# Both products of a feed-forward block by one level of Strassen's recursion, the down product as a phase of its own

## The chip, the core and the metric

The kernel runs on one core of one Trainium2 chip. The metric is the device time of one execution in microseconds: 1386.5, 1390.3 and 1393.4 us in three runs of the kernel before, a median of 1390.3. Engines are named as the profile names them: PE (TensorE matmul) with PEld (its weight loads), DVE (VectorE), ACT (ScalarE), POOL (GpSimd) and SP (SyncE), which here only issues DMAs.

## The reference

The reference is a transformer block on 1024 frames of width 1024 with 16 meta tokens ahead of them: a mixer (retention and attention heads with an output projection), then a gated feed-forward part with a short convolution, then a final norm. The change touches the end of the mixer's output projection, the feed-forward part and the final norm:

```python
def conv_ffn(h, w_up, conv_w, conv_b, w_down, valid):
    up = jnp.einsum('bld,df->blf', h, w_up)
    a, b = jnp.split(up, 2, axis=-1)
    a = a * valid.astype(a.dtype)[None, :, None]
    a_pad = jnp.pad(a, ((0, 0), (CONV_W - 1, 0), (0, 0)))
    acc = conv_b
    for j in range(CONV_W):
        acc = acc + a_pad[:, j:j + L] * conv_w[j]
    return jnp.einsum('blf,fd->bld', jax.nn.silu(acc) * b, w_down)
```

with `h = h + conv_ffn(rms_norm(h, ffn_norm_g), ...)` and `rms_norm(h, final_norm_g)` after it. Everything is float32.

## The kernel before

Activations lie transposed: the 1024 model features are 8 tiles (d or k, 0 to 7) of 128 partitions, the frames are columns. NQ is 1026 columns: the 1024 frames (NF) and the two tokens ahead of them that the convolution needs. The feed-forward width 2816 is 22 tiles (ft) of 128.

PE multiplies in the type fp32r, which keeps fewer digits than float32. So every operand is split into a high part (a cast, on ACT) and a low part (the difference, on DVE or POOL), and each product is three matmuls: high by high, high by low, low by high. Every matmul has its own weight load.

1. Rest of the output projection, in `rest_mm` (L1048): for each d in the order 6, 7, 0, ..., 5, matmuls of 342 columns, three to a row of NQ. Tiles 6 and 7 need all 8 k, the others the last two k, whose weights POOL splits on the way (`load_w`, L118). DVE adds the result to the residual H (`rest_h`, L1054); ACT and DVE make the two halves of H times the norm's weight, `hss` (L1055, L1058); squares are summed in `acc2` (L1063 to L1067).
2. Up product: `up_mm` (L1089) multiplies `hss`, not yet divided by its root mean square. `rstd` (L124 to L128) and a broadcast through DRAM give that factor, `rb2`, and DVE applies it when it reads the product out of PSUM (L1138 for a, L1150 for b). So PE can start the up product before the factor is known.
3. Per ft, `up` then does the convolution (L1141 on ACT, L1142 and L1143 on DVE), Silu (L1144), the gate (L1151) and the split of the result u (L1153, L1154), and loads and splits the down weights.
4. Down product: `down` (L1166 to L1168) multiplies the tile before, ft - 1, eight d by two halves of 512 columns, and DVE adds each result to H in SBUF (L1170). The last two tiles are left for the end, where the final norm works in column chunks of 512, 256 and 256.

The order inside a stage before step 2's loop is written out by hand (`manual_schedule`). From `up(0)` on the framework's scheduler sets the order of all engines. SP's order is the scheduler's throughout.

## Time and profile before

| | us |
|---|---|
| three runs | 1386.5, 1390.3, 1393.4 |
| profiled execution: span from first to last instruction | 1387.9 (the page gives no other time of it) |
| rest of the output projection, first matmul | 563.0 |
| feed-forward part, first matmul (L1089) | 612.1 |
| last down matmul (L1168) | 1368.9 |
| PE busy, DVE busy, ACT busy, POOL busy | 1339.2, 816.7, 464.6, 270.1 |

In the profile a matmul's duration overlaps that of its neighbours, so what a matmul costs in a dense stretch is read from start to start. A stretch of the span is read from a row of busy times: its length, then PE, PEld, DVE, ACT and POOL, the clock that PE was granted (1.00 is full), the busy share of the 16 DMA engines and GB/s. A wait is put down to the instruction that released it.

### The profile page before, as it was taken

What the parts mean: (1) busy time and instruction counts of PE and PEld (TensorE: products, weight loads), DVE (VectorE), ACT (ScalarE), POOL (GpSimd) and SP (SyncE); (2) the same over time, 40 slices, a digit from 0 to 9 for tenths busy, and PEclk for the clock granted to TensorE, in tenths of its full rate; (3) what the DMA queues carried; (4) which work ended last, traced back from release to release, by engine and by line L of the source; (5) the groups of instructions that cost most, each with busy time, mean ns of one, the idle gap of its engine ahead of it and who ended that gap; (6) DMA issues with size and microseconds to landing.
All of it is one profiled execution on the core that took longest, in us unless ns stands there. A gap on an engine that the chain in (4) does not pass through costs nothing.

```text
span 1387.9 us, 20331 instructions
## 1 busy us (share of the span) xinstructions
PE 1339.2 (96%) x8257; PEld 1225.0 (88%) x8257; DVE 816.7 (59%) x1400; ACT 464.6 (33%) x825; POOL 270.1 (19%) x177
## 2 busy tenths in 40 slices
...
GB/s 291 158 97 111 33 74 75 25 65 99 70 95 80 137 154 88 199 83 61 31 46 46 46 46 46 49 59 46 47 55 52 50 56 47 46 46 46 16 0 122
DMA packets 45237, 103.89 MB, mean 75 GB/s; under 512 B 7951, under 2 KB 18527, under 8 KB 45144
## 3 DMA queue, kind: packets, MB, share of 16 engines
...
## 4 chain that ended last, share of the span: by engine, by line
PE 82%; DVE 3%; issue 2%; ACT 2%; POOL 1%; DMA 0%; DVEq 0%; SPq 0%; POOLq 0%; ACTq 0%
PE psj L1089 18%; PE psv L1089 18%; PE psD L667 11%; PE psq L1167 6%; PE psq L1168 6%; PE psq L1166 6%; PE psO L825 4%; PE psD L895 4%; PE psS L788 3%; PE psS L731 2%; PE psj L1048 1%; PE psq L1048 1%; PE psj L185 1%; PE psj L184 1%; PE psj L183 1%
## 5 line engine op out<-in xcount | busy, mean ns | idle before, releaser
L1170 DVE TENSOR_TENSOR H<-H,psq 128x512 f32<-128x512 f32 (+1 forms) x344 | 229.3, 673 | 181.2 <-PE psq L1168 181.2
L1089 PE MATMUL psj<-hs,u_hi 128*128 128x342 f32 x1056 | 222.1, 322 | 2.0 <-ACT u_hi L117 2.0
L1089 PEld LDWEIGHTS psj<-hs,u_hi 128*128 128x128 f32 x1056 | 182.4, 190 | 15.9 <-ACT u_hi L117 2.4
L1089 PE MATMUL psv<-hs,u_hi 128*128 128x512 f32 x704 | 195.8, 398 | 0.0
L1089 PEld LDWEIGHTS psv<-hs,u_hi 128*128 128x128 f32 x704 | 134.1, 191 | 29.5
L1141 ACT ACTIVATE ca<-at,sm 128x1024 f32<-128x1024 f32 x22 | 25.4, 1154 | 369.8 <-DVE at L1138 369.8
L118 POOL TENSOR_TENSOR d_lo<-d_raw,d_hi 128x1024 fp32r<-128x1024 f32 x22 | 52.9, 2404 | 493.0 <-ACT d_hi L117 493.0
L1166 PE MATMUL psq<-u,d_hi 128*128 128x512 f32 (+1 forms) x368 | 141.0, 385 | 2.0 <-ACT u L1153 1.6
L1167 PE MATMUL psq<-u,d_hi 128*128 128x512 f32 (+1 forms) x368 | 141.1, 383 | 0.3 <-DVE u L1154 0.3
L1168 PE MATMUL psq<-u,d_lo 128*128 128x512 f32 (+1 forms) x368 | 141.1, 383 | 0.0
L667 PE MATMUL psD<-xl,f_hi 128*128 128x256 f32 (+2 forms) x448 | 129.7, 290 | 0.0
L667 PE MATMUL psD<-xh,f_hi 128*128 128x256 f32 (+2 forms) x448 | 128.8, 287 | 0.4 <-DVE fq L673 0.4
L667 PE MATMUL psD<-xh,f_lo 128*128 128x256 f32 (+2 forms) x448 | 128.5, 287 | 0.0
L118 POOL TENSOR_TENSOR u_lo<-u_raw,u_hi 128x1024 fp32r<-128x1024 f32 x44 | 107.2, 2437 | 76.0 <-ACT u_hi L117 68.4
L1089 PE MATMUL psv<-hs,u_lo 128*128 128x512 f32 x352 | 114.6, 395 | 0.0
L1089 PE MATMUL psj<-hs,u_lo 128*128 128x342 f32 x528 | 112.3, 320 | 1.0 <-POOL u_lo L118 1.0
L1150 DVE TENSOR_TENSOR bt<-psv,rb 128x512 f32<-128x512 f32 x44 | 28.4, 686 | 115.4 <-PE psv L1089 115.4
L1089 PEld LDWEIGHTS psj<-hs,u_lo 128*128 128x128 f32 x528 | 89.8, 189 | 5.1 <-POOL u_lo L118 1.3
L798 ACT ACTIVATE pf<-psS 128x272 f32<-128x272 f32 (+4 forms) x112 | 49.7, 451 | 116.4 <-PE psS L788 70.6
L667 PEld LDWEIGHTS psD<-xh,f_hi 128*128 128x128 f32 x448 | 85.3, 190 | 0.9 <-DVE fq L673 0.6
L667 PEld LDWEIGHTS psD<-xl,f_hi 128*128 128x128 f32 x448 | 85.0, 190 | 0.4
L667 PEld LDWEIGHTS psD<-xh,f_lo 128*128 128x128 f32 x448 | 85.0, 190 | 0.1
...
## 6 DMA issues: line engine op xcount, KB each, us to landing
...
```

The lines of the kernel that those rows point to most:

```text
L118: eng_lo.tensor_tensor(lo, src, f(hi), op=ALU.subtract)
L667: pe.matmul(ps[:, :n], lhsT=w_, rhs=X(e, k, t0 + a, n), start=(k == 0 and i == 0), stop=(k == KT - 1 and i == 2))
L788: pe.matmul(ps[:r, off:off + n], lhsT=k_[s][:, t0:t0 + r], rhs=q_[s][:, q0:q0 + n], start=(e == 0), stop=(e == 1 and not diag))
L798: act.activation(pf[:r, a:b], ps[:r, a:b], AF.Exp)
L825: pe.matmul(po[:, q0 - qs:qn], lhsT=v_, rhs=P2[:r, P_, off:off + n], start=(i == 0 and e == 0), stop=(fin and e == 2))
L895: pe.matmul(ps[:, :n], lhsT=w_, rhs=mt[k][:, hl, a:a + n], start=(first and k == ks[0] and i == 0), stop=(stop and k == ks[-1] and i == 2))
L1089: pe.matmul(ps[:, :n], lhsT=w_, rhs=hss[k][:, hl, t0 + a:t0 + a + n], start=(ki == 0 and i == 0), stop=(ki == KT - 1 and i == 2))
L1150: dve.tensor_tensor(bt[:, a:a + n], ps[:, :n], rb2[:, 2 + a:2 + a + n], op=ALU.mult)
L1166: pe.matmul(ps[:, :n], lhsT=w_h, rhs=u[:, 0, c0:c0 + n], start=(i == 0), stop=False)
L1167: pe.matmul(ps[:, :n], lhsT=w_h, rhs=u[:, 1, c0:c0 + n], start=False, stop=False)
L1168: pe.matmul(ps[:, :n], lhsT=w_l, rhs=u[:, 0, c0:c0 + n], start=False, stop=(i == len(sts) - 1))
L1170: dve.tensor_tensor(hsl, hsl, ps[:, :n], op=ALU.add)
```

## The change

Strassen's recursion (in Winograd's form) splits both operands of a product into four blocks and forms the product from seven block products instead of eight, at the price of sums of blocks. Here S1 to S4 are sums of weight blocks and T1 to T4 sums of activation blocks; `SEQ` lists the seven pairs, products 0 to 6.

Up product. For each ft, the weight block rows are the two halves of the 1024 features, and its block columns the a half and the b half of the up projection. The frames are two pairs (p = 0, 1) of two blocks of 256 columns (258 where the two extra columns are). A product (`prod`) is 12 matmuls of 256 or 258 columns: 4 k by three. The seven products of a pair accumulate in three PSUM banks (psa, psb, psc, one of each for each pair); between them `post` takes partial results out, two on ACT and five on DVE per pair. POOL forms S1 to S4 per ft (`sums`), ACT and DVE split the seven weight blocks (`unit`), three products ahead (LA).

The activation blocks B11, B21, B22 and T1 to T4 are formed once per pair (`build`), from activations that are already normalised. So the order becomes: rest of the output projection for pair 0, `norm(0)`, rest for pair 1 with `build(0)` in between, then the products of ft = 0 for pair 0 while `norm(1)` and `build(1)` run, then pair 1's. H goes to DRAM (`hsave`) and comes back in the down product.

Down product. Its inner width, 22 tiles, is halved into 11 (KH). Instead of using u at once, the kernel stores u and its T sums in DRAM (`conv2`, `tsum`), along with the S sums of the down weights, which POOL forms half a tile per ft (`sd_sum`). After the last ft the seven products run one after another, 11 steps each, every step with two blocks of 128 x 512 read from DRAM, split on ACT and DVE, and 12 matmuls of 512 columns into four of eight PSUM banks (`d_mm`). The last three steps are done in two halves of 256 columns, and the final norm follows for three column chunks. All this is in one `manual_schedule`; SP is again set by the scheduler.

```diff
+    PAIR = ((0, 514, 258, 2), (514, 512, 256, 0))
...
+    SEQ = (("A11", "B11"), ("S2", "T2"), ("A12", "B21"), ("S3", "T3"), ("S1", "T1"), ("A22", "T4"), ("S4", "B22"))
...
+    def rest_h(p, d, r):
+        c0, cw, _, _ = PAIR[p]
+        for ps, (a, n) in zip(*r):
+            hsl = Hp[p][:, d, a:a + n]
+            dve.tensor_tensor(hsl, ps[:, :n], hsl, op=ALU.add)
+        sp.dma_start(hsave[d][:, c0:c0 + cw], Hp[p][:, d, :])
...
+    def norm(p):
+        starts = [0, 128, 256, 384] + ([386] if p == 0 else [])
+        ps = bank(px)
+        m = len(starts)
+        for j, s_ in enumerate(starts):
+            pe.matmul(ps[:, j:j + 1], lhsT=accs[p][:, s_:s_ + P], rhs=ones, start=True, stop=True)
+        r = wo.tile([P, 5], F32, tag="fr", name="fr", bufs=2)[:, :m]
+        act.activation(r, ps[:, :m], AF.Sqrt, bias=epsc, scale=1.0 / 1024)
+        dve.reciprocal(r, r)
...
+        def tsub(nm, x, y):
...
+            v = tt[-1][:, :1024] if nm in ("T1", "T3") else tt[-1][:, 1024:2048]
...
+            dve.tensor_tensor(v, x, y, op=ALU.subtract)
+            return v
+        def tput(nm, v):
+            t = b_tile(p, nm)
+            hi(t, v)
+            return lambda: lo(t, v, dve)
+        for d in range(2):
+            hn(d)
+        yield
+        for d in range(2, 4):
+            hn(d)
+        raw("B11", 0, 0, n)
+        yield
+        T1 = tsub("T1", B12, B11)
+        hn(4)
+        hn(5)
+        yield
+        hn(6)
+        hn(7)
+        yield
+        T2 = tsub("T2", B22, T1)
+        t2 = tput("T2", T2)
+        yield
+        raw("B21", 1, 0, n)
+        yield
+        if p == 0:
+            T3 = tsub("T3", B22, B12)
+            t2()
+            yield
+            t3 = tput("T3", T3)
+            t1 = tput("T1", T1)
+            T4 = tsub("T4", B21, T2)
+            t4 = tput("T4", T4)
+            raw("B22", 1, c2, 256)
+            yield
+            t3()
+            yield
+            t1()
+            yield
+            t4()
+            yield
...
+            t1 = tput("T1", T1)
+            t2()
+            t1()
+            yield
+            T3 = tsub("T3", B22, B12)
+            tput("T3", T3)()
+            yield
+            T4 = tsub("T4", B21, T2)
+            tput("T4", T4)()
+            yield
+            raw("B22", 1, c2, 256)
+            yield
...
+    def raw_load(ft, pl):
...
+        for hf in range(2):
+            sp.dma_start(raws[ft][hf].rearrange("p a b -> p (a b)"), wup[ft, :, hf * 1024:(hf + 1) * 1024])
...
+    def sums(ft, nm):
+        r0, r1 = raws[ft]
...
+        t = Wr.tile([P, 512], F32, tag=nm, name=nm)
+        x, y, o = {"S1": ("A21", "A22", ALU.add), "S2": ("S1", "A11", ALU.subtract),
+                   "S3": ("A11", "A21", ALU.subtract), "S4": ("A12", "S2", ALU.subtract)}[nm]
+        pool.tensor_tensor(t, s_[x], s_[y], op=o)
+        s_[nm] = t
...
+    def split_u(t, src, eng):
+        act.copy(t[:, 0], src)
+        eng.tensor_tensor(t[:, 1], src, f(t[:, 0]), op=ALU.subtract)
...
+    def prod(ft, i, p):
+        nm = SEQ[i][1]
+        n = 258 if p == 0 and i in (0, 2) else 256
+        key = (ft, p, "ababcbc"[i])
+        new = i in (0, 1, 4)
+        if new:
+            BK[key] = bank({"a": pa, "b": pb, "c": pc}[key[2]])
+        ps = BK[key]
+        w, o = units_u[ft, i], ops[p][nm]
+        for k in range(4):
+            for j, (wi, hl) in enumerate(((0, 0), (0, 1), (1, 0))):
+                pe.matmul(ps[:, :n], lhsT=w[:, wi, k * P:(k + 1) * P], rhs=o[:, hl, k, :],
+                          start=(new and k == 0 and j == 0), stop=(k == 3 and j == 2), skip_group_check=not new)
+    s1t, ats, bts = {}, {}, {}
...
+    def post(ft, i, p):
+        c0, _, n, off = PAIR[p]
+        B_ = lambda x: BK[ft, p, x][:, off if x == "a" else 0:][:, :256]
+        fr = 512 * p
+        if i == 0:
+            s1t[p] = Wu.tile([P, 256], F32, tag=f"s1{p}", name="s1")
+            act.copy(s1t[p], B_("a"))
+        elif i == 1:
+            if p == 0:
+                ats[ft] = Wu.tile([P, NQ], F32, tag="at", name="at")
+            at = ats[ft]
+            dve.tensor_tensor(at[:, c0 + n:c0 + n + 256], B_("b"), s1t[p], op=ALU.add)
+        elif i == 2:
+            act.copy(ats[ft][:, c0:c0 + n], BK[ft, p, "a"][:, :n])
+        elif i == 3:
+            if p == 0:
+                bts[ft] = stage("bt")[:, :NF]
+            dve.tensor_tensor(bts[ft][:, fr + 256:fr + 512], B_("b"), s1t[p], op=ALU.add)
+        elif i == 4:
+            x = bts[ft][:, fr + 256:fr + 512]
+            dve.tensor_tensor(x, B_("c"), x, op=ALU.add)
+        elif i == 5:
+            dve.tensor_tensor(bts[ft][:, fr:fr + 256], B_("b"), s1t[p], op=ALU.add)
+        else:
+            x = ats[ft][:, c0 + n:c0 + n + 256]
+            dve.tensor_tensor(x, B_("c"), x, op=ALU.add)
+    cas, us = {}, {}
...
+    def tsum(ft):
+        u = us.pop(ft)
+        kt = ft % KH
...
+            tg = "T2" if nm == "T1" else nm
+            t = po_s.tile([P, 512], F32, tag=f"{tg}o", name=f"{nm}o")
+            dve.tensor_tensor(t, x, y, op=ALU.subtract)
+            sp.dma_start(u_d[nm][kt], t)
+            return t
+        if ft < KH:
+            one("T1", u[:, 1], u[:, 0])
+        else:
+            o = old.pop(kt)
+            t2 = one("T2", u[:, 1], o[:, 0])
+            one("T3", u[:, 1], o[:, 1])
+            one("T4", u[:, 0], t2)
...
+    def sd_sum(ft):
+        kt, hf = divmod(ft, 2)
+        A11, A21, A12, A22 = (sdt[0][:, i] for i in range(4))
+        S1, S2, S3, S4 = (sdt[1][:, i] for i in range(4))
+        pool.tensor_tensor(S1, A21, A22, op=ALU.add)
+        pool.tensor_tensor(S2, S1, A11, op=ALU.subtract)
+        pool.tensor_tensor(S3, A11, A21, op=ALU.subtract)
+        pool.tensor_tensor(S4, A12, S2, op=ALU.subtract)
+        for nm, t in zip(("S1", "S2", "S3", "S4"), (S1, S2, S3, S4)):
+            sp.dma_start(s_d[nm][kt][:, 256 * hf:256 * hf + 256], t)
...
+    def d_mm(g, j, c, n, new):
+        i, kt = divmod(g, KH)
+        a_, b_ = d_units[g, 0], d_units[g, 1]
+        ps = (X, Y)[i in (1, 3, 5)][j]
+        for m, (wi, hl) in enumerate(((0, 0), (0, 1), (1, 0))):
+            pe.matmul(ps[:, c:c + n], lhsT=a_[:, wi, j * P:(j + 1) * P], rhs=b_[:, hl, c:c + n],
+                      start=(new and m == 0), stop=(kt == KH - 1 and m == 2), skip_group_check=i in (2, 3, 5, 6))
...
+        mm = rest_mm(1, 0, 6, wo_w(6))
+        next(mm)
+        nrm = norm(0)
+        next(nrm)
+        r = next(mm)
+        mm = rest_mm(1, 1, 7, wo_w(7))
+        bld = build(0, next(nrm))
+        next(mm)
+        rest_h(1, 6, r)
+        r = next(mm)
+        next(bld)
+        next(bld)
+        rest_h(1, 7, r)
...
+        unit(0, 2)
+        prod(0, 0, 0)
+        for d in range(6):
+            rest_sq(1, d, dve)
+            if d == 1:
+                next(bld)
+        sums(0, "S3")
+        sums(0, "S4")
+        prod(0, 1, 0)
+        post(0, 0, 0)
+        nrm = norm(1)
+        next(nrm)
+        unit(0, 3)
+        for _ in bld:
+            pass
+        prod(0, 2, 0)
+        post(0, 1, 0)
+        bld = build(1, next(nrm))
+        sd_buf = xp.tile([P, KT * 272], F32, tag="x0", name="sd", bufs=2)
+        next(bld)
+        next(bld)
+        unit(0, 4)
+        lastp = [(2, 0)]
+        for x, (i, p) in enumerate([(3, 0), (4, 0), (0, 1), (1, 1), (5, 0), (2, 1), (6, 0),
+                                    (3, 1), (4, 1), (5, 1), (6, 1)], 1):
+            prod(0, i, p)
+            post(0, *lastp.pop())
+            next(bld, None)
+            if x <= 3:
+                next(bld, None)
+            if x == 3:
+                unit(0, 5)
+            if x == 4:
+                unit(0, 6)
+            if x == 7:
+                for _ in bld:
+                    pass
+                ho.close()
+                po_ = mk(bo, "po", side="right")
+                raw_load(1, po_)
+                sums(1, "S1")
+                sums(1, "S2")
+            if x >= 9:
+                unit(1, x - 9)
+            if x == 10:
+                sums(1, "S3")
+            lastp.append((i, p))
...
+        for ft in range(1, NFT):
+            pl = (Wr, po_s)
+            for i in range(7):
+                for p in range(2):
+                    prod(ft, i, p)
+                pf, pi = (ft, i - 1) if i else (ft - 1, 6)
+                if (pf, pi) == (0, 6):
+                    post(0, *lastp.pop())
+                else:
+                    for p in range(2):
+                        post(pf, pi, p)
+                if i == 0:
+                    conv1(ft - 1)
+                    if ft + 1 < NFT:
+                        raw_load(ft + 1, pl[(ft + 1) % 2])
+                    if ft >= KH:
+                        t_load(ft - KH)
+                if i == 1:
+                    conv2(ft - 1)
+                    sums(ft, "S4")
+                if i == 2:
+                    tsum(ft - 1)
+                if i == 5:
+                    sd_sum(ft - 1)
+                    sd_load(ft)
+                g = 7 * ft + i + LA
+                if g < 7 * NFT:
+                    unit(*divmod(g, 7))
+                else:
+                    d_unit()
+                if ft + 1 == NFT and 1 <= i < 6:
+                    d_load(i)
...
+        def d_post(i, j):
+            ps = (X, Y)[i in (1, 3, 5)][j]
...
+                act.copy(s1d[j], ps)
+                for d, c in ((j, H1), (4 + j, H0), (4 + j, H1)):
+                    pool.tensor_tensor(H[d][:, c], H[d][:, c], s1d[j], op=ALU.add)
+                return
+            for d, c in {1: [(j, H1)], 2: [(j, H0)], 3: [(4 + j, H1)], 4: [(4 + j, H1)], 5: [(4 + j, H0)]}[i]:
+                dve.tensor_tensor(H[d][:, c], ps, H[d][:, c], op=ALU.add)
...
+        for g in range(7 * KH):
+            i, kt = divmod(g, KH)
+            if i < 6 or kt < KH - NL:
+                for j in range(4):
+                    d_mm(g, j, 0, 512, i in (0, 1, 4) and kt == 0)
+            if i and kt == 0:
+                for j in range(4):
+                    d_post(i - 1, j)
+            if i == 0 and 2 <= kt < KT + 2:
+                with tc.issue_after(d_last[0].ins):
+                    sp.dma_start(H[kt - 2], hsave[kt - 2][:, 2:])
+            if i == 1 and kt == 4:
...
+            for _ in range(3):
+                if d_next[0] < 2 * (g + 5):
+                    d_unit()
```

PE, from the end of the rest for pair 1 to ft = 0 for both pairs. B0 and B1 are the blocks of the two pairs (B0T and B0B with numbers: T2, B21 and so on in the order of `SEQ`), fu and unit the split weight blocks, L1098 and L1111 the two parts of `norm(1)`.

```order
L1064 MATMUL psb<-m_6387,wo_7586 128x512 x3
L1250 MATMUL psa<-B0B_7958,fu 128x258 x12
L1250 MATMUL psb<-B0T_8018,fu 128x256 x12
L1098 MATMUL psx<-ones,acc_8000 128x1 x4
L1250 MATMUL psa<-B0B_8029,unit 128x258 x12
L1111 MATMUL psx<-dg,on 128x128 x4
L1250 MATMUL psb<-B0T_8055,unit 128x256 x12
L1250 MATMUL psc<-B0T_8057,unit 128x256 x12
L1250 MATMUL psa<-B1B_8168,fu 128x256 x12
```

Before, the first up matmuls followed the last rest matmul directly:

```order
L1048 MATMUL psq<-m_6387,wo_l 128x342 x3
L1089 MATMUL psj<-hs_7576,u_hi 128x342 x6
L1089 MATMUL psj<-hs_7576,u_lo 128x342 x3
L1089 MATMUL psj<-hs_7577,u_hi 128x342 x6
L1089 MATMUL psj<-hs_7577,u_lo 128x342 x3
L1089 MATMUL psj<-hs_7570,u_hi 128x342 x6
```

Now the norm's matmuls stand in PE's queue between the second and third product of pair 0.

DVE at the same place, from T2 of pair 0 on: L1148 forms a T, L1132 makes a low half, L1226 splits a weight block, L1076 is a residual addition and L1089 a sum of squares for pair 1.

```order
L1148 TENSOR_TENSOR tt<-Hp_7571,tt 128x1024
L1076 TENSOR_TENSOR Hp_7572<-psb,Hp_7572 128x512
L1226 TENSOR_TENSOR fu<-S_7987,fu 128x512
L1076 TENSOR_TENSOR Hp_7572<-psa,Hp_7572 128x512
L1148 TENSOR_TENSOR tt<-Hp_7571 128x1024
L1132 TENSOR_TENSOR B0T_8018<-tt,B0T_8018 128x1024
L1076 TENSOR_TENSOR Hp_7572<-psb,Hp_7572 128x512
L1148 TENSOR_TENSOR tt<-Hp_7571,tt 128x1024
L1226 TENSOR_TENSOR unit<-u_raw,unit 128x512
L1089 TENSOR_TENSOR acc_8000<-sq_8085,acc_8000 128x512
L1089 TENSOR_TENSOR acc_8000<-sq_8088,acc_8000 128x512
L1132 TENSOR_TENSOR B0T_8055<-tt,B0T_8055 128x1024
```

The squares on which `norm(1)` waits stand behind T3, T2's low half and T4.

DVE in one of the later ft, from the convolution of the tile before to the additions of product 3 (L1272): L1305 is the gate, L1266 the additions of product 1, L1318 the T differences for the down product.

```order
L1290 SCALAR_TENSOR_TENSOR ca<-at,sm,ca 128x1024
L1226 TENSOR_TENSOR unit<-S_12154,unit 128x512
L1305 TENSOR_TENSOR u<-bt,ca 128x1024
L1226 TENSOR_TENSOR unit<-S_12048,unit 128x512
L1266 TENSOR_TENSOR at<-psb,s_12224 128x256
L1266 TENSOR_TENSOR at<-psb,s_12226 128x256
L1318 TENSOR_TENSOR T2o<-u,old 128x512
L1318 TENSOR_TENSOR T3o<-u,old 128x512
L1318 TENSOR_TENSOR T4o<-u,T2o 128x512
L1226 TENSOR_TENSOR unit<-u_raw,unit 128x512
L1226 TENSOR_TENSOR unit<-S_12233,unit 128x512
```

Before, the gate stood between additions out of PSUM:

```order
L1142 SCALAR_TENSOR_TENSOR ca<-at,sm,ca 128x1024
L1143 SCALAR_TENSOR_TENSOR ca<-at,sm,ca 128x1024
L1170 TENSOR_TENSOR H_7566<-H_7566,psq 128x512
L1150 TENSOR_TENSOR bt<-psv,rb_8078 128x512 x2
L1170 TENSOR_TENSOR H_7559<-H_7559,psq 128x512
L1151 TENSOR_TENSOR bt<-bt,ca 128x1024
L1170 TENSOR_TENSOR H_7559<-H_7559,psq 128x512
```

Now most of what stands ahead of the additions that a product needs has both inputs in SBUF.

486 lines of the change are left out of this document (312 added, 174 removed).

## The prediction

> **What bounds the kernel now.** I read the page first, then the busy times of the stages, then the chain and the order in time of the feed-forward part.
>
> ```profile
> span 1387.9 us, 20331 instructions
> PE 1339.2 (96%) x8257; PEld 1225.0 (88%) x8257; DVE 816.7 (59%) x1400; ACT 464.6 (33%) x825; POOL 270.1 (19%) x177
> PE 82%; DVE 3%; issue 2%; ACT 2%; POOL 1%; DMA 0%; DVEq 0%; SPq 0%; POOLq 0%; ACTq 0%
> ```
> ```profile
> 900.00:1200.00 300.00, 300.00 (x1503) 263.26 (x1502) 172.22 (x225) 56.53 (x53) 62.50 (x27) 1.00 0.15 48
> ```
> ```profile
> 726.08 1.86 PE psv L1089 x8
> ...
> 1331.24 1.86 PE psv L1089 x8
> ```
>
> TensorE is 82% of the chain that ended last. In the middle of the feed-forward part (columns: stretch, length, busy PE, PEld, DVE, ACT, POOL, granted clock, DMA share, GB/s) PE has no idle moment and its full clock, while DVE is busy 57%. The two chain rows are the same place of the loop 18 passes apart: (1331.24 - 726.08)/18 = 33.62 us for each of the 22 feed-forward tiles. So only fewer or cheaper matmul columns shorten this stage, as long as DVE keeps up.
>
> **What one matmul costs.** Start to start, not the overlapping durations:
>
> ```profile
> 903.55 0.39 PE L1166 MATMUL psq<-u,d_hi 128*128 128x512 f32 x1
> ...
> 905.60 0.32 PE L1089 MATMUL psj<-hs,u_hi 128*128 128x342 f32 x1
> ```
> ```profile
> 301.43 0.28 PE L667 MATMUL psD<-xl,f_hi 128*128 128x256 f32 x1
> ...
> 302.02 0.28 PE L667 MATMUL psD<-xh,f_hi 128*128 128x256 f32 x1
> ```
> ```profile
> L667 PEld LDWEIGHTS psD<-xh,f_hi x448: 186/188/334, 191.1 to 462.1; 128*128 128x128 f32 x150
> ```
> ```profile
> 563.02 1.11 PE L1048 MATMUL psj<-m,f_hi 128*128 128x342 f32 x6
> ...
> 577.75 1.10 PE L1048 MATMUL psq<-m,f_hi 128*128 128x342 f32 x6
> ...
> 589.08 1.10 PE L1048 MATMUL psj<-m,wo_h 128*128 128x342 f32 x6
> ```
>
> Nine of 512 columns take 2.05 us: 0.228 each. Five steps of 256 columns take 0.59: 0.118 each, although every one has its own weight load of 188 ns; the loads overlap. 72 of 342 columns take 589.08 - 577.75 = 11.33: 0.157 each. The new size, 256, therefore costs no more per column than half of 512 plus 4 ns.
>
> **The terms on PE.** From the first matmul of the output projection's rest (563.0) to the last feed-forward matmul (1368.87, row below) are 806.1 us, and 18.8 us of tail follow. Of these, before: rest 252 x 0.157 = 39.7; attention matmuls in between, 14.7 - 11.3 = 3.4; 22 x 33.62 = 739.6. That is 782.7, so 23.4 us are stalls and slow clock.
>
> After, with the counts of the built order: rest 168 x 0.118 + 84 x 0.228 = 39.0; attention 3.4; up 22 x 7 x 2 x 12 = 3696 of 256 (258), 436.1; down 888 of 512 and 72 of 256, 210.8. Sum 689.3, which is 93.4 less. What has to be seen is how much comes back as waiting.
>
> **What DVE, ACT and POOL have to do.** Rows for the prices (min/median/max ns, or start and duration in us):
>
> ```profile
> L118 DVE TENSOR_TENSOR f_lo<-f_raw,f_hi x48: 418/683/1558, 40.5 to 569.3; 128x512 fp32r<-128x512 f32 x42, 128x256 fp32r<-128x256 f32 x6
> L118 POOL TENSOR_TENSOR sl<-sf,sh x36: 454/725/946, 51.9 to 190.2; 128x256 fp32r<-128x256 f32 x16, 128x128 fp32r<-128x128 f32 x16, 16x258 fp32r<-16x258 f32 x4
> L118 POOL TENSOR_TENSOR rv_lo<-rv_raw,rv_hi x8: 1272/1296/1363, 72.1 to 85.2; 128x512 fp32r<-128x512 f32 x8
> L1154 DVE TENSOR_TENSOR u<-bt,u x22: 1211/1225/2207, 645.6 to 1344.4; 128x1024 fp32r<-128x1024 f32 x22
> L1142 DVE SCALAR_TENSOR_TENSOR ca<-at,sm,ca x22: 1277/1280/1286, 637.6 to 1331.9; 128x1024 f32<-128x1024 f32 x22
> L1170 DVE TENSOR_TENSOR H<-H,psq x344: 399/689/691, 670.1 to 1372.8; 128x512 f32<-128x512 f32 x164, 128x256 f32<-128x256 f32 x8
> L1203 DVE SCALAR_TENSOR_TENSOR fo<-H,sm,psv x14: 469/472/741, 1366.3 to 1383.5; 128x256 f32<-128x256 f32 x13, 128x512 f32<-128x512 f32 x1
> L1153 ACT CAST u<-bt x22: 1044/1054/1056, 644.5 to 1343.3; 128x1024 fp32r<-128x1024 f32 x22
> ```
> ```profile
> 1027.32 1.15 ACT L1141 ACTIVATE ca<-at,sm 128x1024 f32<-128x1024 f32 x1 [17.43 <-DVE at L1138]
> ```
> ```profile
> 1005.33 2.40 POOL L118 TENSOR_TENSOR u_lo<-u_raw,u_hi 128x1024 fp32r<-128x1024 f32 x1 [0.40 <-PE psq L1168]
> ```
> ```profile
> 1005.59 0.68 DVE L1170 TENSOR_TENSOR H<-H,psq 128x512 f32<-128x512 f32 x1
> 1006.18 2.63 DVE L1151 TENSOR_TENSOR bt<-bt,ca 128x1024 f32<-128x1024 f32 x1
> ```
> ```profile
> 602.38 1.71 POOL L118 TENSOR_TENSOR wo_l<-wo_raw,wo_h 128x256 fp32r<-128x256 f32 x1
> ```
> ```profile
> 600.20 3.30 DVE L1058 SCALAR_TENSOR_TENSOR hs<-H,sm,hs 128x1026 fp32r<-128x1026 f32 x1
> ```
>
> The last four fences show the trap. While POOL works from 1005.33 to 1007.73, a DVE addition with one input in PSUM takes its usual 0.68, but a product of two SBUF tiles takes 2.63 instead of the 1.23 of L1154. At 602.38 it is POOL that takes 1.71 instead of 0.73, behind a DVE instruction. They take turns, each for a whole instruction.
>
> Up, per tile: PE 168 x 0.118 = 19.8 us. DVE: 7 splits x 0.68, 10 PSUM additions x 0.40, two convolution steps x 1.28, the gate 1.23 as in L1154, one T difference x 0.68 in tiles 0 to 10 and three in 11 to 21: 13.2 and 14.6 us. POOL: four sums x 1.30 and four x 0.73: 8.1 us. If DVE stood still for all of POOL's time, a tile would need 21.3 and 22.7, a mean of 22.1; if never, PE's 19.8. Those are the bounds: 0 to 2.3 us of excess per tile. Where it sits: after pair 1's last product, DVE adds (0.40), ACT scales (1.15), DVE does two steps (2.56), ACT's Silu (1.15), the gate (1.23), a split (0.68), then the two additions of product 1 (0.80), all in one queue: 8.0 us, with an allowance of 0.1 of signalling at each of four handovers 8.4. PE needs the first of these additions at its fourth product pair, 6 x 12 x 0.118 = 8.5 us on. It just fits. Behind them come the T differences and two splits, then the additions of product 3, due at 14.2; POOL's sums begin about then, since its S1 waits for DVE's split of the old S1. Taking turns (POOL 1.1 and 0.6, DVE 0.55 each behind the other) I get 13 for one T and 14.7 for three. So 0 in the first half, 0.5 to 1 in the second: 0.5 as a mean over all, because the first chain has no slack either. 21 x 0.5 = **10 us** (0 to 48). ACT, with seven half-size casts, two activations and four small copies, has some 8 us per tile and is no bound.
>
> **The start of the up product.** Before, the norm's factor came after the matmul; now the normalised operand has to exist first. From the end of pair 0's rest at about 588, DVE must do 8 residual additions x 0.69, 16 scalings x 0.74, 16 instructions of 1024 columns x 1.23, 13 of 512 x 0.68, 9 diagonals and some PSUM additions: 50 us. PE has 19.2 of pair 1's rest and 19.8 of tile 0 to do meanwhile. DVE's sum alone leaves PE idle 14 us. Laid out queue by queue, PE waits more: 7.6 us for T2's low half before product 1 (two scalings, T1, T2, ACT's 1.05, T3 are ahead of it); then 10.4, because norm(1)'s four small matmuls stand in PE's queue ahead of product 2 and need all of pair 1's squares, which DVE does behind T4; 7 around the second half of norm(1), whose diagonal is queued behind T1's and T4's low halves; 5.6 for T2 of pair 1; and some 5 in single microseconds. 36 in all.
>
> ```profile
> 600.00:604.00 4.00, 1.64 (x11) 1.34 (x9) 3.96 (x3) 2.96 (x4) 3.96 (x2) 1.00 0.00 1
> ```
> ```profile
> 608.00:616.00 8.00, 5.82 (x25) 5.54 (x26) 7.95 (x7) 3.87 (x5) 6.75 (x3) 0.79 0.43 135
> ```
>
> Stretches in which PE idled are followed by one at a lower clock: 8 us at 0.79, 1.7 us lost. Three such gaps: 5. Together **41 us** (14 to 57, the upper end with the other 16 us of POOL's work there blocking DVE too).
>
> **Up to down, the down product, the tail.** The last tile's additions, convolution, gate and three T (8.5 us with ACT's two parts) and up to 2.4 of POOL's turns stand on DVE ahead of the two splits for the third step (1.4): 10 to 12 us against the 2 x 12 x 0.228 = 5.5 that the two prepared steps last. **5 us** (2 to 12). Then a step takes 2.74 on PE, 1.4 on DVE and 1.1 on ACT, and streams two blocks of 0.262 MB: 192 GB/s.
>
> ```profile
> 0.00:34.70 34.70, 31.72 (x231) 29.47 (x231) 20.35 (x56) 26.26 (x58) 2.89 (x19) 1.00 0.88 291
> 480.00:500.00 20.00, 18.34 (x120) 18.03 (x119) 10.52 (x19) 10.44 (x22) 0.00 (x0) 0.91 0.66 176
> ```
>
> Scaled to a full share these are 331 and 267 GB/s. While H comes back in eight steps the demand doubles to 383, so the queue falls up to 9.5 us behind, but the loads run some eight steps (22 us) ahead. **0** (0 to 10). The Trainium skill (SBUF — State Buffer, The DMA setup-cost knee) says that each transfer pays about 2 us of its own, so that blocks of 256 KiB reach 224 GB/s and larger ones should be preferred. By it, an estimate, a step's blocks take 2.34 us and those with H 4.7, up to 16 us late before the lead is counted: the same 0 for the sum. No row here shows the rate of such blocks alone; the first row, 291 GB/s, is above it.
>
> ```profile
> 1368.87 0.28 PE L1168 MATMUL psq<-u,d_lo 128*128 128x256 f32 x1
> ...
> 1381.53 2.44 DVE L1203 SCALAR_TENSOR_TENSOR fo<-H,sm,psv 128x256 f32<-128x256 f32 x6 [1.64 <-ACT prs L1191]
> ```
>
> The tail loses its wait for POOL (most of the middle chunk is summed earlier): add, square, sum 1.4; first emits 2.8; norm 1.5; emits 2.4; and the 3.9 from those rows to the end: **12** instead of 18.8 (10 to 19).
>
> **Sum.** 563.0 + 689.3 + 41 + 10 + 5 + 0 + 12 = 1320. The page gives no time beside its span, and the median of the runs, 1390.3, is 2.4 above it. Forecast: **1323 us**. All lower bounds together give 1281, all upper ones 1401.
>
> **The rivals.**
> A: DVE becomes the bound in the up product, since it and POOL exclude each other. For it: the 2.63 row, and 13 of DVE's 23 instructions in a later tile have two SBUF inputs. Against: the ten PSUM additions pass, and POOL can run while DVE waits for ACT. A tile takes 22.1: 1323 + 21 x 1.8 = 1361. The Trainium skill (SBUF — State Buffer, Who interferes with whom) says that a DVE instruction with two SBUF inputs and a GpSimd one reading SBUF exclude each other for the whole instruction. By that rule, the rows agree.
> B: the hand layout is too pessimistic; only DVE's sum counts at the start and the up loop hides all: 1323 - 27 - 10 = 1286.
> C, slower: the down product is bound by its stream from DRAM. It decides above 67/77 = 0.87 us more per step, thus under 0.524 MB / 3.61 us = 145 GB/s; at 130 GB/s a step takes 4.03 and the time is 1323 + 77 x 1.29 = 1422. For it: small blocks, one queue in which a load stands behind stores that wait for DVE and POOL. Against: 291 GB/s in the first row above.
> D: the columns saved are not time because each weight load takes 188 ns: excluded by 0.118.
>
> **How the numbers follow.** Forecast 0.60, A 0.17, B 0.12, C and other slow mechanisms 0.08, no change 0.03. Faster: 0.60 + 0.17 + 0.12 = 0.89; within 0.5% (what a measurement here can just tell) 0.03; slower 0.08. The forecast's own range is 1300 to 1346; taking in A and part of B, 1294 to 1368.
>
> **What would show it.** PE spacing of 0.118 in the products; a tile period of 20 to 21 us, with PE's gaps ahead of products 3 and 5; 30 to 45 us of PE idle between 590 and 665; down steps of 2.74 at a DMA share of 0.6 to 0.7. Wrong if the period is over 21.5 (A), or if PE waits for DMA in the down product (C).

## The result

The changed kernel takes 1351.2 us (median of 1345.1, 1349.8, 1352.5 and 1356.9) against 1391.8 for the kernel before on the same chip: a ratio of 0.970, 95% interval 0.966 to 0.975. It is faster, as forecast, and 28 us slower than the forecast of 1323: inside the range of 1294 to 1368, just outside the forecast's own 1300 to 1346.

The page of the changed kernel (span, busy times, chain):

```profile
span 1348.0 us, 24030 instructions
PE 1263.3 (94%) x9187; PEld 1196.1 (89%) x9187; DVE 925.0 (69%) x1564; ACT 584.3 (43%) x1153; POOL 367.2 (27%) x309
PE 72%; DVE 7%; issue 4%; ACT 3%; DMA 3%; POOL 1%; SPq 0%; DVEq 0%; POOLq 0%; ACTq 0%
```

PE is busy 76 us less than before, DVE 108 us more. DVE, ACT, DMA and "issue" have grown in the chain, so PE waits more. Where, the busy times of stretches show (length, then PE, PEld, DVE, ACT, POOL, granted clock, DMA share, GB/s):

```profile
588.00:677.07 89.07, 56.06 (x289) 49.51 (x290) 60.90 (x82) 26.64 (x39) 24.90 (x14) 0.75 0.25 85
613.97:677.07 63.10, 32.40 (x186) 30.01 (x185) 45.15 (x52) 21.74 (x31) 17.29 (x9) 0.68 0.17 59
721.89:901.47 179.58, 179.58 (x1515) 179.58 (x1514) 145.97 (x189) 67.67 (x117) 89.37 (x72) 1.00 0.45 146
922.32:1089.12 166.80, 161.53 (x1347) 160.14 (x1345) 145.38 (x184) 60.10 (x104) 83.54 (x65) 1.00 0.57 189
1122.00:1300.00 178.00, 178.00 (x785) 147.39 (x784) 113.56 (x160) 87.51 (x158) 28.16 (x20) 1.00 0.64 211
```

The first row runs from the rest of the output projection for pair 1 to the end of tile 0 (the up product of ft = 0): PE is busy 56 of 89 us, at a granted clock of 0.75. The second is tile 0 alone. The third is nine tiles of the first half, without any gap: 179.58 / 9 = 19.95 us a tile, 0.1188 per matmul. The fourth is eight tiles of the second half, where u's three T differences are formed: 20.85 us each, 0.66 of them a gap. The last is the down product, again without a gap, at 0.64 of the DMA engines.

PE in order of time, from pair 1's rest to the end of tile 0 (start, duration, and in brackets the idle time ahead and what ended it):

```profile
590.30 1.12 PE L1064 MATMUL psa<-m,f_hi 128*128 128x512 f32 x2 [3.54 <-DVE Hp L1076]
...
613.97 1.59 PE L1250 MATMUL psa<-B0B,fu 128*128 128x258 f32 x12
617.27 0.38 PE L1250 MATMUL psb<-B0T,fu 128*128 128x256 f32 x1 [1.70 <-ACT fu L1225]
622.66 2.72 PE L1250 MATMUL psb<-B0T,fu 128*128 128x256 f32 x11 [5.01 <-DVE B0T L1132]
636.78 1.84 PE L1098 MATMUL psx<-ones,acc 128*128 128x1 f32 x8 [11.40 <-DVE acc L1089]
638.48 2.93 PE L1250 MATMUL psa<-B0B,unit 128*128 128x258 f32 x12
...
643.29 0.49 PE L1111 MATMUL psx<-dg,on 128*128 128x128 f32 x2 [1.05 <-DVE dg L1105]
...
648.20 0.58 PE L1250 MATMUL psc<-B0T,unit 128*128 128x256 f32 x2 [2.98 <-ACT unit L1225]
650.71 2.50 PE L1250 MATMUL psc<-B0T,unit 128*128 128x256 f32 x10 [1.94 <-DVE unit L1226]
...
657.03 0.39 PE L1250 MATMUL psb<-B1T,fu 128*128 128x256 f32 x1 [1.41 <-ACT B1T L1129]
658.29 2.38 PE L1250 MATMUL psb<-B1T,fu 128*128 128x256 f32 x11 [0.87 <-DVE B1T L1132]
664.47 0.80 PE L1250 MATMUL psb<-B0T,unit 128*128 128x256 f32 x2 [3.80 <-ACT unit L1225]
665.81 2.50 PE L1250 MATMUL psb<-B0T,unit 128*128 128x256 f32 x10 [0.55 <-DVE unit L1226]
...
677.07 1.60 PE L1250 MATMUL psa<-B0B,unit 128*128 128x258 f32 x12
```

In tile 0 the idle times add up to 30.7 us; those of 11.40 and 5.01 are the two largest. Twelve matmuls take 2.93 us behind the long gap, 1.59 in tile 0's first row.

The third step of the down product, where it starts to wait, and its end:

```profile
1116.19 0.51 PE L1399 MATMUL psa<-d_u 128*128 128x512 f32 x1 [1.14 <-ACT d_u L1225]
1119.56 2.50 PE L1399 MATMUL psa<-d_u 128*128 128x512 f32 x5 [2.86 <-DVE d_u L1226]
...
1306.00 0.95 PE L1607 MATMUL nps<-ones,ac 128*128 128x1 f32 x8
1307.84 1.16 PE L1615 MATMUL pr<-dg,on 128*128 128x128 f32 x8 [0.89 <-DVE dg L1614]
...
1321.76 1.58 PE L1399 MATMUL psa<-d_u 128*128 128x256 f32 x11 [1.00 <-DVE d_u L1226]
...
1327.66 0.61 PE L1607 MATMUL nps<-ones,ac 128*128 128x1 f32 x4
1330.66 0.81 PE L1615 MATMUL pr<-dg,on 128*128 128x128 f32 x4 [2.40 <-DVE dg L1614]
1331.13 3.90 PE L1399 MATMUL psc<-d_u 128*128 128x256 f32 x18
```

Two of the final norm's chunks (L1607, L1615) stand in PE's queue between product matmuls, and the last 18 of these take 3.90 us, nearly twice the 18 x 0.118 = 2.1 us of the prediction's price.

Against the forecast's sum:

| part | forecast | measured |
|---|---|---|
| first matmul of the output projection's rest | 563.0 | 562.5 |
| rest and tile 0 (62.2 on PE + 41) | 103.2 | 114.5 |
| tiles 1 to 21 (416.3 + 10) | 426.3 | 432.4 |
| up to down, down product (210.8 + 5) | 215.8 | 225.6 |
| tail | 12 | 13.0 |
| span | 1320.3 | 1348.0 |

So 11 us went in the start, 6 in the tiles, 10 in the down product.

### The profile page after: what moved, and what is told of

Same layout as the page of the kernel before. It is cut to its first block, busy times and chain, and to the rows that moved or that the text cites. A ratio compares the mean times of both kernels' runs of the same rounds, so it can differ in the third digit from the quotient of the medians.

```text
span 1348.0 us, 24030 instructions
## 1 busy us (share of the span) xinstructions
PE 1263.3 (94%) x9187; PEld 1196.1 (89%) x9187; DVE 925.0 (69%) x1564; ACT 584.3 (43%) x1153; POOL 367.2 (27%) x309
## 4 chain that ended last, share of the span: by engine, by line
PE 72%; DVE 7%; issue 4%; ACT 3%; DMA 3%; POOL 1%; SPq 0%; DVEq 0%; POOLq 0%; ACTq 0%
PE psb L1250 13%; PE psD L667 11%; PE psc L1250 8%; PE psa L1250 8%; PE psc L1399 4%; PE psO L825 4%; PE psa L1399 4%; PE psD L895 3%; PE psx L1399 3%; PE psb L1399 3%; PE psS L788 2%; PE psS L731 2%; PE psj L185 1%; PE psa L1064 1%; PE psj L184 1%
## 5 line engine op out<-in xcount | busy, mean ns | idle before, releaser
L1226 DVE TENSOR_TENSOR d_u<-d_raw,d_u 128x512 fp32r<-128x512 f32 x154 | 117.6, 816 | 60.5 <-ACT d_u L1225 60.5
L1225 ACT CAST d_u<-d_raw 128x512 fp32r<-128x512 f32 x154 | 87.3, 619 | 98.1 <-PE psc L1399 47.5
L1250 PE MATMUL psb<-B0T,unit 128*128 128x256 f32 x780 | 106.7, 287 | 12.5 <-ACT unit L1225 9.7
L1250 PEld LDWEIGHTS psb<-B0T,unit 128*128 128x128 f32 x780 | 99.3, 193 | 15.0 <-issue 6.6
L1250 PE MATMUL psb<-B1T,unit 128*128 128x256 f32 x780 | 103.2, 282 | 0.0
L1250 PEld LDWEIGHTS psb<-B1T,unit 128*128 128x128 f32 x780 | 97.5, 190 | 0.0
L1226 DVE TENSOR_TENSOR unit<-S,unit 128x512 fp32r<-128x512 f32 x87 | 87.6, 1007 | 4.6 <-ACT unit L1225 4.6
L1226 DVE TENSOR_TENSOR unit<-u_raw,unit 128x512 fp32r<-128x512 f32 x65 | 79.8, 1228 | 3.6 <-ACT unit L1225 3.6
L1288 ACT ACTIVATE ca<-at,sm 128x1024 f32<-128x1024 f32 x22 | 25.3, 1151 | 125.1 <-DVE at L1280 125.1
L183 PE MATMUL psj<-rv_hi,xh 128*128 128x256 f32 (+1 forms) x264 | 76.8, 295 | 1.6 <-DVE z L287 1.2
L185 PE MATMUL psj<-rv_hi,xl 128*128 128x256 f32 (+1 forms) x264 | 76.4, 292 | 0.0
```

The costliest lines, as they stand in the source:

```text
L183: pe.matmul(ps[:, :w], lhsT=x_h, rhs=w_h[:, c0:c0 + w], start=(k == 0), stop=False)
L185: pe.matmul(ps[:, :w], lhsT=x_l, rhs=w_h[:, c0:c0 + w], start=False, stop=(k == KT - 1))
L1225: act.copy(t[:, 0], src)
L1226: eng.tensor_tensor(t[:, 1], src, f(t[:, 0]), op=ALU.subtract)
L1250: pe.matmul(ps[:, :n], lhsT=w[:, wi, k * P:(k + 1) * P], rhs=o[:, hl, k, :], start=(new and k == 0 and j == 0), stop=(k == 3 and j == 2), ...
```

## The experiments

The attention part ahead of the change ended between 562 and 571 us in the runs' traces, with the same instructions, and single times of one kernel differ by up to 12 us. By the ratios to the kernel before, only the combined run at the end is told apart from the change; the intervals of the other runs overlap with its own. Stages are therefore compared inside each trace, of which every run has one, from the start of their first matmul (us):

| run | tile 0 | tile 1 | tiles 2-11 | tiles 12-21 | down | tail | median of runs | ratio to before, interval |
|---|---|---|---|---|---|---|---|---|
| the change | 63.1 | 24.9 | 199.5 | 208.0 | 225.6 | 13.0 | 1351.2 | 0.970 (0.966 to 0.975) |
| e1_norm_later | **65.9** | 22.7 | 199.5 | 207.8 | 225.5 | 13.0 | 1349.7 | 0.970 (0.968 to 0.972) |
| e2_squares_pool | **61.6** | 22.2 | 199.5 | 207.7 | 225.5 | 13.0 | 1349.1 | 0.969 (0.967 to 0.972) |
| e3_sums_early | 63.6 | 22.2 | 199.5 | **212.9** | 226.0 | 13.0 | 1355.5 | 0.973 (0.971 to 0.975) |
| e4_norm_split | 63.5 | 22.8 | 199.5 | 207.9 | **224.3** | **15.2** | 1349.1 | 0.968 (0.966 to 0.971) |
| e5_sums_gap | 63.3 | 25.3 | 199.5 | **203.6** | 225.6 | 13.0 | 1347.6 | 0.970 (0.968 to 0.972) |
| e6_start_order | **68.6** | **20.0** | 199.7 | 208.2 | 225.1 | 13.2 | 1350.3 | 0.972 (0.970 to 0.975) |
| e7_keep_clock | **63.3** | 24.8 | 199.5 | 207.6 | 225.5 | 13.0 | 1349.9 | 0.971 (0.968 to 0.975) |
| e8_end_order | 63.5 | 22.5 | 199.5 | 207.6 | **220.5** | **14.7** | 1346.0 | 0.968 (0.966 to 0.970) |
| e9_combined | **57.0** | **22.4** | 199.5 | **203.7** | **220.5** | **15.1** | 1336.7 | 0.961 (0.960 to 0.963) |
| e10_no_pool_lows | **60.5** | 23.7 | 199.5 | 207.9 | 225.4 | 13.0 | one: 1349.9 | |
| e11_sums_twice | 63.4 | 24.9 | **199.5** | **208.9** | 227.5 | 12.9 | one: 1355.5 | |
| e12_stream_twice | 63.4 | 22.9 | 199.5 | 207.7 | **231.9** | **45.2** | one: 1387.8 | |

Bold is what an edit touches. Where nothing was edited, tile 0 takes 63.1 to 63.6 us, tiles 2 to 11 199.5 to 199.7 and the down product 225.1 to 226.0 (227.5 in e11, see there). Tile 1 varies more: it takes 22 to 23 or about 25.

The traces tell these two apart. In all runs but e6, e9 and e10, POOL's sums for tile 1 begin when the tile's weights have landed: 2.4 to 3.3 us ahead of the tile where it takes 22.2 to 22.9 us, 1.9 to 2.0 ahead where it takes 24.8 to 25.3 us. In the latter PE waits 0.7 to 0.8 us ahead of product 2 (at most 0.3 in the others), and its matmuls are slow behind the wait that follows. No run moved the landing by itself. In the changed kernel:

```profile
683.69 1.72 PE L1250 MATMUL psa<-B0B,unit 128*128 128x258 f32 x12 [0.79 <-ACT s L1261]
688.93 2.55 PE L1250 MATMUL psb<-B0T,unit 128*128 128x256 f32 x12 [2.10 <-DVE at L1266]
```

### The start: whose queue?

**norm(1) later in PE's queue.** In the prediction norm(1)'s small matmuls, in front of product 2, cost 10.4 us.

```diff
         post(0, 0, 0)
+        prod(0, 2, 0)
         nrm = norm(1)
...
-        prod(0, 2, 0)
         post(0, 1, 0)
```

> On PE alone, product 2 of pair 0 goes ahead of norm(1)'s four small matmuls; no other queue changes. In the changed kernel PE waited 11.4 us there (625.4 to 636.78) with product 2's operands ready at about 629.2. Theory of the prediction (the small matmuls in PE's queue cost 10.4 us): product 2 is out of the way while DVE does the squares, PE has 1.4 to 2.9 us less behind the wait, and the first tile ends 3 to 8 us earlier than 677.07: total 1343 to 1348. Rival (DVE's own queue sets this stretch, and PE's place in it is free): the second half of norm(1) still waits for its fourth diagonal on DVE at 643.24, the first scaling of pair 1 stays at 643.8, the first tile ends at 676.5 to 677.5: total unchanged within 1 us of 1351.

Neither: tile 0 becomes 2.8 us longer. PE of this run:

```profile
636.08 2.95 PE L1250 MATMUL psa<-B0B,unit 128*128 128x258 f32 x12 [10.63 <-ACT s L1261]
638.82 1.70 PE L1098 MATMUL psx<-ones,acc 128*128 128x1 f32 x8
```

And ACT of the changed kernel, before product 2 started there:

```profile
635.07 0.63 ACT L1088 ACTIVATE sq<-Hp 128x512 f32<-128x512 f32 x1 [0.17 <-DVE acc L1089]
635.61 0.35 ACT L1261 COPY s<-psa 128x256 f32<-128x256 f32 x1
```

Product 2 was not ready at 629. It adds into the bank of product 0, which ACT has to copy out first, and that copy stands behind pair 1's squares in ACT's queue, which wait for DVE's additions one by one. So the gap was forecast in size and place, but PE's order was not its cause. With product 2 in front, norm(1) comes 2 us later, and with it everything of pair 1.

**Squares off DVE.** The six additions of pair 1's squares go to POOL, each behind its residual addition.

```diff
             rest_h(1, d, r)
             next(bld)
...
+            rest_sq(1, d, pool)
...
-        for d in range(6):
-            rest_sq(1, d, dve)
...
```

> The squares' additions of pair 1 go from DVE (six, 629.08 to 636.6) to POOL, each right behind its residual addition. Nothing is left out. Theory DVE's queue: DVE loses 6.5 us of work and 2.9 us of waiting, norm(1) can start at about 627 instead of 636.8, and the first tile ends 7 to 11 us earlier: total 1340 to 1344. Rival, turn-taking: POOL's six additions of 1.3 us each block DVE's scalings and differences in 608 to 626 for up to 1.3 us each, B0's low halves on POOL come later by as much, and no more than 2 us are left of the gain: total 1349 to 1352.

Near the rival: 1.5 to 2 us of tile 0, not 7 to 11. The last square still stood behind the casts of T3, T1, T4 and B22 on ACT and behind a low half on POOL. Tile 0 of this run:

```profile
618.44:680.00 61.56, 35.65 (x184) 32.99 (x185) 42.56 (x46) 21.05 (x30) 25.52 (x15) 0.64 0.18 60
```

DVE has six instructions less and is busy 42.6 instead of 45.2 us, but idle 19.0 instead of 18.0.

**Clock.** PE's gaps are filled with matmuls nobody needs.

```diff
         prod(0, 0, 0)
+        keep(48)
...
         post(0, 0, 0)
+        keep(80)
```

with 24, 12 and 30 more ahead of three later products; `keep(m)` multiplies the first unit by B11 m times.

> Some 190 matmuls of 256 columns that compute nothing needed stand in PE's gaps of tile 0, so that PE doesn't idle there; everything else is unchanged. Theory of the prediction (slow clock behind the gaps costs 5 us): the products take 0.118 per matmul again, and tile 0 takes 58 to 60 instead of 63.1. Rival (PE waits for DVE anyway, the slow clock hides in those waits): products are as fast as that, but tile 0 takes 61.5 to 63.5.

PE of this run:

```profile
628.14 1.57 PE L1250 MATMUL psb<-B0T,fu 128*128 128x256 f32 x11 [1.34 <-DVE B0T L1132]
629.55 9.59 PE L1470 MATMUL psc<-B0B,fu 128*128 128x256 f32 x80
642.36 1.02 PE L1098 MATMUL psx<-ones,acc 128*128 128x1 f32 x8 [3.23 <-DVE acc L1089]
643.25 2.90 PE L1250 MATMUL psa<-B0B,unit 128*128 128x258 f32 x12
```

Product 1's rest takes 1.57 us instead of 2.72, the norm's matmuls 1.02 instead of 1.84 (product 2, behind a gap of 3.2 us, is still slow). Over tile 0 the granted clock is 0.92 instead of 0.68, and tile 0 stays at 63.3. A slow matmul ahead of a wait only shortens the wait: the 5 us for slow clock were no term of the path, and PE's speed is not what sets tile 0.

**POOL's low halves left out.** The low halves of B11, B21 and B22 are not computed; ACT fills them with copies.

```diff
             hi(t, src)
-            lo(t, src, pool)
+            act.copy(t[:, 1], src)
```

> Leaves out part of the computation: the low halves of B11, B21 and B22 of both pairs, which POOL computes as differences (six of 2.4 us), are replaced by copies on ACT, so that the operands' low halves hold the high ones. POOL's share of tile 0 falls by 14.5 us, ACT's grows by 6.3. In the changed kernel five of DVE's instructions between 617 and 661 took 1.4 to 1.8 us more than the same kind alone (2.49, 2.25 and 2.48 against 0.68 for a split, 1.76 against 0.69 for an addition, 2.65 against 1.23), each beside one of POOL's. Theory turn-taking (these turns are on the chain): tile 0 takes 54 to 58 us instead of 63.1 to 63.6. Rival (DVE's own sum and its waits for ACT's casts set the length; POOL only fills them): 60.5 to 63.5.

The busy times of this run, from pair 1's rest on and in tile 0, to be held against the first two rows of the stretches above:

```profile
592.12:678.62 86.50, 56.99 (x293) 49.98 (x292) 53.78 (x82) 32.70 (x46) 11.60 (x9) 0.78 0.27 91
618.09:678.62 60.53, 34.04 (x185) 31.68 (x186) 37.40 (x52) 26.84 (x37) 3.37 (x4) 0.69 0.19 61
```

In tile 0 DVE does the same 52 instructions in 37.4 instead of 45.2 us: 7.8 us were turns with POOL. Tile 0 falls by 2.6 to 3.1 us only, at the rival's edge, since DVE's idle time grows from 18.0 to 23.1. ACT's extra copies (its busy time grows by 5.1) may hide a part of the gain; how much was not tested. So turn-taking is the smaller part, and DVE's busy time is not what sets tile 0 either. Every operand goes from DVE to ACT (high half) and back to DVE or POOL (low half), and what is saved of DVE's work comes back for the most part as waiting for the other engines.

**Order in the second half of tile 0.** Units 5 and 6, the low half of pair 1's B22 and tile 1's raw weights earlier, and products 5 and 6 of pair 0 ahead of pair 1's product 1.

```diff
-        for x, (i, p) in enumerate([(3, 0), (4, 0), (0, 1), (1, 1), (5, 0), (2, 1), (6, 0),
+        for x, (i, p) in enumerate([(3, 0), (4, 0), (0, 1), (5, 0), (6, 0), (1, 1), (2, 1),
...
-            if x == 3:
-                unit(0, 5)
-            if x == 4:
-                unit(0, 6)
+            if x == 1:
+                unit(0, 5)
+                unit(0, 6)
+                raw_load(1, Wr)
...
```

> Tile 0: units 5 and 6, the low half of pair 1's B22 and the raw weights of tile 1 come earlier, and on PE products 5 and 6 of pair 0 stand ahead of product 1 of pair 1. Same work and the same sum on DVE. Theory order (what ended late was held by ACT's and POOL's queues and by the weights' load issued at 667 us): tile 0 falls from 63.1 to 58 to 60, tile 1 from 24.9 (22.2 to 22.8 in the runs beside it) to 20.0 to 21.5; total 1343 to 1346. Rival (DVE's sum sets the end): tile 0 stays above 62; tile 1 22 or more; total 1349 or more.

Split: tile 1 takes 19.95 us, as the theory has it, and tile 0 is 5.5 us longer, which no theory had. PE, DVE and POOL of this run:

```profile
667.88 2.93 PE L1249 MATMUL psa<-B1B,unit 128*128 128x256 f32 x12 [6.39 <-ACT s L1260]
675.53 2.93 PE L1249 MATMUL psb<-B1T,unit 128*128 128x256 f32 x12 [4.72 <-DVE at L1265]
```
```profile
663.23 3.25 DVE L1148 TENSOR_TENSOR sd<-Hp 128x1024 f32<-128x1024 f32 x1
```
```profile
659.65 5.75 POOL L1132 TENSOR_TENSOR B1B<-Hp,B1B 128x1024 fp32r<-128x1024 f32 x2 [9.10 <-ACT B1B L1129]
665.36 2.25 POOL L1220 TENSOR_TENSOR S<-u_raw 128x512 f32<-128x512 f32 x1
```

With its weights there early, tile 1's sums on POOL fell beside T3 and T4 of pair 1 on DVE: 3.25 us instead of 1.23 for one difference, 2.25 instead of 1.3 for one sum. And PE's new order made products wait for copies out of PSUM that kept their place behind casts. In the changed kernel the load was late, as its chain of waits shows:

```profile
668.02 6.96 DMA u_raw<-wup
```

Both tiles together take 88.5 us, within the 85.8 to 88.6 of the runs with an unedited start: some 5 us moved from tile 1 to tile 0.

### The second half of the up product

**POOL's sums elsewhere.** First they went behind S3.

```diff
-                if i == 5:
-                    sd_sum(ft - 1)
-                    sd_load(ft)
...
                         sums(ft + 1, {3: "S1", 4: "S2", 6: "S3"}[i])
+                if i == 6:
+                    sd_sum(ft - 1)
+                    sd_load(ft)
```

> The four sums on POOL for the down product (4 x 1.18 us per tile) move from behind S1 and S2, where DVE does the T differences and two splits, to the place behind S3, where POOL had 10.3 us idle in every tile. Same work. Theory turn-taking: in tiles 12 to 21 the two splits ahead of PE's wait take 0.68 again instead of 1.22, the gap of 0.66 us and the slower matmuls behind it go, the period falls from 20.85 to 19.95: ten tiles x 0.9 = 9 us, total 1341 to 1344. Rival (the three T differences are DVE's own work and too much for the place): period stays 20.6 to 20.9, total 1349 to 1352. Third: the moved sums now block the convolution steps, period above 20.9 and a gap ahead of product 3.

They missed the idle stretch, which lies ahead of S1:

```profile
951.65 1.29 POOL L1221 TENSOR_TENSOR S<-u_raw 128x512 f32<-128x512 f32 x1 [10.89 <-DVE unit L1226]
```

S3, twice as wide as one of the moved sums, now ran beside DVE's T4, and a tile took 21.40. Behind S4 (`if i == 1`) they really lie in that stretch:

> The four sums for the down product stand behind S4 in POOL's queue, thus really in the stretch of 10.3 us in which POOL waited for DVE's release of the old S1 (behind S3, as in the run before, they were still behind that wait). Same work. Theory turn-taking (POOL's additions beside DVE's differences and splits cost the 0.9 us per tile): tiles 12 to 21 take 19.95 to 20.1 us instead of 20.85, that stage 200 to 201 us instead of 208, total 1342 to 1345. Rival (DVE's own work with three differences): 206 to 208, total 1350. Third (the sums now block the two convolution steps): first half above 19.95 too.

20.32 us a tile, ten tiles 4.3 us less, all in the direction of turn-taking and half its size. In this run the two splits ahead of PE's wait take 0.68 us again, as forecast; T3 and T4 still meet S2 and S3:

```profile
961.12 1.78 DVE L1318 TENSOR_TENSOR T4o<-u,T2o 128x512 f32<-128x512 f32 x1
962.83 0.68 DVE L1226 TENSOR_TENSOR unit<-u_raw,unit 128x512 fp32r<-128x512 f32 x1
```

With the same work on DVE and POOL, a tile takes 1.45, 0.90 or 0.37 us more than 19.95, by the place of POOL's sums alone. No run left the sums out, so how much of the 0.37 is DVE's own (two more T differences than in the first half) is not shown.

**The sums twice.**

```diff
+        for _ in range(2):
             pool.tensor_tensor(S1, A21, A22, op=ALU.add)
...
```

> Each of the four sums for the down product is computed twice by POOL, at the place that it has in the changed kernel (4 x 0.73 to 1.18 us more per tile); nothing else changes. It asks where the prediction's rival A begins. Rival A's rule (DVE and POOL exclude each other, and the loop has no slack): every tile 2 to 4.7 us longer, the first half at 22 to 24.5 instead of 19.95, the second at 23 to 25.5 instead of 20.85. The prediction's layout (POOL's work can fall where DVE waits, the place decides): first half 19.95 to 21, second half 21.5 to 23.

Nothing per tile: 19.95 and 20.85 us still, at or below the lowest that either theory gave (1 us is added once in the last tile, and 2 at the start of the down product). The second set, some 3.7 us, falls behind DVE's two splits, where PE waits for nothing. So what rival A is about is not the sum of both engines' work, at least not up to that much more.

### The down product

**Norms split.** The second halves of the first two norms later in PE's queue (`f_norm` in two parts, the second called one step later and behind the last matmuls).

> In the down product the second halves of the first two final norms (the matmuls with the diagonals) move in PE's queue behind one more step (first norm) and behind the last 18 matmuls (second norm). Same work. Theory (PE's own queue order costs here): the waits of 0.9 and 2.4 us and the slow clock behind the second (18 matmuls in 3.9 instead of 2.1 us) go: the last product matmul comes 4 to 5 us earlier and the total falls by 3 to 5: 1346 to 1348. Rival (the end is set by DVE's and POOL's emission of the output): total unchanged within 1 us.

The product ends 1.3 us earlier, the tail is 2.3 longer. The first norm's wait is gone, and PE gains 1.0 us there, but DVE's last splits come 2.0 us later in the stage, and PE waits 2.68 us for them instead of 1.00, with slow matmuls behind. Of these 2.0 us PE had lost 1.3 already ahead of the edit, with slow matmuls behind the stage's first waits. In both kernels the splits stand beside POOL's products of the output: six of them take 9.2 to 9.3 us, more than twice the 0.68 each that a split takes alone.

**End in another order.** The first norm comes one step earlier, and the additions of squares one place later.

```diff
-                if kt == 3:
-                    f_norm(0)
+                if kt == 2:
+                    for _ in f_norm(0):
+                        pass
...
-                sq_add(1 + hf, j)
+                add()
+                add = sq_add(1 + hf, j, True)
...
```

with the second half of `f_norm(1)` behind the last product matmul; `add` is the addition that a square leaves for the next step.

> End of the down product: the first final norm one step earlier, so that ACT and DVE don't stand 6.5 and 4.3 us in front of PE's small matmuls; the second norm's second half behind the last product matmul; the additions of squares one place later, so that DVE doesn't wait 0.54 us for each of ACT's squares. Same work. Theory queue order: the wait for the last splits (1.0), the norm's waits (0.9, 2.4) and the slow matmuls behind it go; the down product takes 220 to 222 instead of 225.6, the tail stays 13 or grows by 1: total 1346 to 1348. Rival: the splits of the last three steps stay late because POOL's products of the output take turns with them (1.7 instead of 0.7 us each): 224 to 226, total 1350.

As the theory: 5.1 us off the product, 1.7 more in the tail. PE of this run:

```profile
1322.98 1.57 PE L1399 MATMUL psa<-d_u 128*128 128x256 f32 x11 [0.61 <-DVE d_u L1226]
...
1329.11 2.39 PE L1399 MATMUL psc<-d_u 128*128 128x256 f32 x18
1333.38 0.71 PE L1619 MATMUL pr<-dg,on 128*128 128x128 f32 x4 [1.88 <-DVE dg L1618]
```

The gain is at the second norm: the last 18 matmuls no longer wait behind it, nor run slow. The first norm's 0.89 us and the late last splits hardly changed (0.89 and 0.61), so that part of the theory has nothing behind it.

**The stream twice.**

```diff
+                if g >= 14:
+                    ex = dp[0].tile([P, 512], F32, tag="extra", name="extra", bufs=2)
+                    sp.dma_start(ex, d_src(DSEQ[i][x], kt))
```

> From the 15th step of the down product on every block is also read a second time from DRAM into a tile that nothing uses: 1.05 MB per step instead of 0.524, everything else unchanged. It asks how far the stream was from being the bound (the prediction's rival C). From the changed kernel's shares (202 GB/s at a share of 0.61, 322 at 0.93) the ceiling is 331 to 346 GB/s: steps of 3.0 to 3.2 us instead of 2.72, down product 242 to 260 us instead of 225.6. If blocks of 256 KB flowed at the 224 GB/s that the Trainium skill (SBUF — State Buffer, The DMA setup-cost knee) gives as a figure for them: steps of 4.7 us, down product about 350 us. If more than 383 GB/s flow: unchanged.

The demand was not doubled as meant: the two buffers let the extra reads fall behind, and the rest of them ran in the tail (45 us), ahead of the output's stores in the same queue. But while both ran (first row; the second is the changed kernel in the same stretch):

```profile
1200.00:1300.00 100.00, 100.00 (x442) 82.79 (x442) 54.90 (x85) 45.52 (x79) 4.11 (x3) 1.00 0.89 300
1200.00:1300.00 100.00, 100.00 (x443) 82.84 (x442) 60.43 (x93) 49.95 (x91) 8.85 (x7) 1.00 0.58 185
```

300 GB/s in blocks of 256 KB, against 185 in the changed kernel, and PE has no gap. The Trainium skill (SBUF — State Buffer, The DMA setup-cost knee) gives 224 GB/s for such blocks; the measurement here, with a stream of loads that runs ahead of PE, is above it. The ceiling itself was not reached: the share of the DMA engines is 0.89. The down product is 6.3 us longer, but PE waits for no block: it loses the time at the first norm, where it waits 4.54 us for POOL's sum of squares.

### Put together

Squares on POOL with ACT's squares ahead of the build's casts; the second unit of tile 0 a step earlier; units 5 and 6 and tile 1's raw weights earlier; POOL's sums behind S4; the end as above. The order of the products stays.

> Three edits of separate stages together, same work. Start: the squares' additions of pair 1 on POOL with ACT's squares ahead of the casts of the build, the second first-tile unit one step earlier, units 5 and 6 and tile 1's raw weights earlier (the order of the products as in the changed kernel). Tiles: POOL's sums for the down product behind S4. End: as in the run on the end's order. Theory (DVE's waits for ACT and POOL in the start are what is left, each stage's gain stands by itself): tiles 0 and 1 together 79 to 82 us (86 to 88.6 with DVE's squares, 83.7 with the first form of POOL's), tiles 12 to 21 203.6, down 220.5, tail 14.7; total 1335 to 1340. Rival (DVE and POOL take turns, so that work moved from the one to the other in the start blocks it there): tiles 0 and 1 together 84 to 88; total 1341 to 1345.

1336.7 us, as the theory: 0.961 of the kernel before (interval 0.960 to 0.963) where the change alone has 0.970, thus some 13 us faster than the change. Tiles 0 and 1 together take 79.3 us, and the gains of the other two stages are those of the single runs. Tile 0:

```profile
622.51:679.50 56.99, 34.77 (x185) 31.91 (x186) 44.34 (x47) 21.14 (x31) 27.01 (x14) 0.67 0.19 65
```

DVE is nearly as busy as in the changed kernel (44.3 us against 45.2), but idle 12.6 us instead of 18.0: most of the 6 us are waits of DVE that went, not work taken off it. Which of the start's edits carries them was not taken apart. Tile 1 takes 22.4 us although its weights were there early, in contrast to the 19.95 of the run on the order: here its sums stand in POOL's queue behind pair 1's last low half and begin 3.9 us ahead of the tile, there 13.1.

## Why the prediction was right or wrong

- **PE's terms: right.** 256 columns cost 0.1188 (forecast 0.118), a down step 2.72 (2.74), and no weight load shows. These carried the gain: the sum has 93 us less on PE, and the kernel is 40 us faster, since 53 come back as waits, slow matmuls and the norms' small ones.
- **Start, 41 us: too small by 11, and built wrongly.** The sum of the listed gaps (36) was close: 30.7 in tile 0 and 3.5 ahead of pair 1's rest. The two largest are right, 6.7 (7.6) and 11.4 (10.4), though the cause of the second was wrong: product 2's bank, not PE's order. That the rest of the list fits is luck: 7 around norm(1)'s second half is 1.05, 5.6 for pair 1's T2 is 2.3, and 9.3 us of waits for the weight blocks of products 4 and 5 stand nowhere in it but for "some 5 in single microseconds". "Plus 5 of slow clock" was wrong in kind: of the 52.3 us beyond the 62.2 on PE, the 18 that are no gaps are slow clock and small matmuls, and removing much of the slow clock gains nothing. What should have been priced is the chain through the queues of DVE, ACT and POOL that makes the operands. The prediction took 50 us of work for DVE from 588 on; it is 60.9, of which 7.1 are turns with POOL (53.8 in the run without its low halves), and waits for the other engines come on top: it is idle 18.0 us in tile 0 alone. Work taken off DVE shortens tile 0 by 1.5 to 3 us, less than the work; the 6 us of the combined run are mostly waits. PE's clock and norm(1)'s place in its queue gain nothing. (The lower bound of 14 doesn't follow from the prediction's own numbers: 50 less 19.2 and 19.8 is 11.)
- **Excess in the tiles, 10 us: 16.** "0 in the first half, 0.5 to 1 in the second" came true: the first half's 0.13 is PE's own spacing without a gap, the second half has 1.0. The gap stands ahead of product 5 alone, not of 3 and 5. The reason given, turns with POOL, is shown for the 0.53 us that the sums' place behind S4 takes back. Left out was tile 1, 5 us over: its weights' load waited for pair 1's space, and its sums on POOL began only 2 us ahead of the tile. It runs at 19.95 where they begin 13.1 ahead; the load early alone does not do it (22.4 in the combined run).
- **Up to down, 5: right in size.** The gaps are 1.14 and 2.86 us, with some slow matmuls behind them. But the chain there passes through a store of T4 and a load of u, so DVE's queue was not the only cause; no run tested it:

```profile
1105.31 5.58 DMA uT<-T4o
1110.90 6.12 DMA d_raw<-uB
```

- **Down product, 210.8: too small by 9.8.** The sum held the products alone. The norms' matmuls that stand between them, the waits for their diagonals and the slow clock behind were no term, and the one late split (1.0) wasn't either. A better order takes back 5.1 of it, 3.4 net.
- **Tail, 12: 13.**
- **Rival A** (tile 22.1) didn't happen. The two engines do take turns, but the time of a tile is not the sum of their work, as the doubled sums show; with the sums at a bad place a tile takes 21.4, near A's sign of 21.5. That A's time, 1361, is near the result is chance. **Rival B** (waits hidden) fails at the start. **Rival C** fails: PE had no gap with 300 GB/s flowing instead of 185.

Some things remain open: of DVE's 11 us beyond the 50 at the start the runs name 7; which of the start's edits removes DVE's waits was not tested one by one; and why tile 1's weights land earlier in some executions than in others was not found.
